# A hybrid decoder layer on one core: the attention's output projection as seven block products, and the stretch behind the attention laid out from tasks

## The chip, the cores and the metric

The kernel runs on 1 core of one Trainium2 chip. The time is the device time of one execution in microseconds, and a kernel's time is the median over its runs. Names of the engines: PE is TensorE (PEld its weight loads), DVE is VectorE, ACT is ScalarE, POOL is GpSimd, SP is SyncE, which issues most DMAs here.

## The reference, cut to what matters

One layer for 512 tokens of width 1024, in float32:

```
h = RMSNorm(x)
[q | k | v | x_rnn | g_rnn | gate_attn | gate_rnn] = h @ W_in
A = differential attention (q and k normalised, shared relative bias, causal), 8 heads of 128 columns
R = GeLU(g_rnn) * RG-LRU(CausalConv4(x_rnn))
x = x + (sigmoid(gate_attn) * (A @ P_attn) + sigmoid(gate_rnn) * (R @ P_rnn)) @ W_out
x = x + relu(RMSNorm(x) @ W_up)^2 @ W_down
```

P_attn, P_rnn and W_out are 1024 x 1024, W_up 1024 x 4096, W_down 4096 x 1024. The change is about `A @ P_attn` and about what is computed between the attention and `@ W_out`.

## The kernel before, in words

**Layout and precision.** Activations lie with the model's width on the partitions and the 512 tokens on the free axis. Each matmul operand is split into a high part (a copy rounded to fp32r, made by ScalarE) and a low part (what is left, by VectorE), and `mm3` (L138) makes a product of three matmuls, high x high, high x low, low x high. The weights come as units of 128 x 1024 floats (512 KB). `Weights.fetch` (L99) has SP load one into one of two `wraw` buffers, `cast` (L106) makes the high part `whi` and the low part `wlo` in one of four slots, and a `wraw` buffer is free for the next load when its low part is made. There are two such streams, `wa` (q, k, v, the gate projections, then P_attn) and `wb` (x_rnn and g_rnn, then P_rnn and W_out); they share buffers and slots.

**Order.** ScalarE, VectorE and GpSimd are called through `InOrder` (L61), so each executes its instructions in the order in which the code emits them; what they record has line L69. Each engine waits at its head instruction with all others queued behind it. TensorE's order is the code's, too.

**Stages.** First the norm and the first gates. Then `attention` (L581): 32 steps, one per head and block of 128 queries, then some more to run out. `acts` holds for each step what is done; heads' projections (`qkv_pair`, L502, one per pair of heads) and the gate projections `ga` are generators from which `fill_in` (L195) takes pieces to keep TensorE at work beside the softmax. `normed_a` and `normed_b` normalise q and k: VectorE sums squares (`ss`, `ms`), GpSimd takes the power -1/2 (`rs`, 128 x 8), VectorE multiplies (`qn`); the halves of q and k change places by DMAs of GpSimd (`qkT`). When a head is through, `post_a` (L654) has ScalarE copy its output from PSUM (`of`) and square it (`osq`), `post_b` has TensorE sum it over partitions with a matmul by `ones` (L666) and GpSimd take the power, `post_c` fetches that power to all partitions (`rb`), and `post_d` scales the head into `aT[h]`, high and low.

Then the **recurrent stretch** (pool `rp`, from about 285 to 500 us): for each of four chunks of 256 channels the products for x_rnn and g_rnn (`cols_proj`, 2 units each), the convolution, GeLU, two gate matmuls per block, and the scan. Its order is written by hand: small jobs are put in `side`, `tick` (L907) takes one after each half unit of TensorE work, and fills in with `fill`, the rest of the gates and then `y_attn` (L846), which is A @ P_attn. `y_attn` takes four groups of 256 output columns, each of 2 units x 8 products of 3 matmuls with 512 columns: 8 units, 192 matmuls, `acc<-aT,whi` and `acc<-aT,wlo` in the profile. When the jobs are done, `y_rnn` (L854) makes R @ P_rnn and merges it with the gated attention part into `mT`. During this stretch GpSimd makes sums of W_up's blocks in DRAM (`weight_sums`, L283), 18 loads into or added onto `sum` and 12 writes, each waiting for the one before; they are for the MLP.

**The MLP**, and W_out before it, stand behind this. The MLP's products are made by a seven-product scheme (Strassen-Winograd: a 2 x 2 block product with 7 instead of 8 block products, from sums of blocks), and its order is laid out by a planner from tasks (`task`, L1034). Neither is changed.

PSUM has 8 banks of 128 x 512 floats: pool `ppa` for the attention (3 `acc`, 5 `at`), `ppb` for the recurrent stretch (6 `acc`, 2 `at` for the small gate matmuls), `ppc` from W_out on (8 `acc`).

Of the kernel before, what the change touches and what calls it, by code (L numbers as in the profile page):

```python
# [39 lines left out]
def tile_block(ctx: ExitStack, tc: tile.TileContext, x, w_in, w_rga, w_rgx, w_pa, w_pr, w_o,  # L40
# [38 lines left out]
    def psum(tag):  # L79
        return pp.tile([P, 512], F32, tag=tag, name=tag, bufs=nb[tag])  # L80
# [7 lines left out]
    class Weights:  # L88
# [4 lines left out]
        def cols(self, w, c0, shift=0, k0=0, n=KT):  # L93
            for k0 in range(k0, k0 + n, 4):
                self.reqs.append((w[k0 // 4, c0 // 256], 4))
                self.shift.append(shift)
            return self

# [157 lines left out]
    OQ, OK_, OV, OX, OG, OGA, OGR = (j * DM for j in range(7))  # L256
    wa = Weights(2, 2)
# [7 lines left out]
    for j in range(4):  # L265
        wa.cols(w_pa, 256 * j, 64)
# [3 lines left out]
    for u in range(2):  # L270
        for j in range(2):
            wb.cols(w_pr, 256 * j, 64, 4 * u, 4)
    for j in range(2, 4):
        wb.cols(w_pr, 256 * j, 64)
# [7 lines left out]

    def weight_sums(behind):  # L283
        t = stg.tile([P, 1024], F32, name="sum")
        G.tensor_copy(t[:, :1], behind[:, :1])
        for n in range(2, 8, 2):
            for blocks in (((0, None), (1, "M5"), (3, "M6"), (2, "M4")), ((1, None), (3, "M7"))):
# [12 lines left out]

    def gate_out(dst, j, ps, rb=None):
        u = unit("gate", F32)
        for c in range(2):
# [5 lines left out]
            dst[2 * j + c] = u[:, c, :]  # L309

# [191 lines left out]
    def qkv_pair(j, qk, v):  # L502
# [22 lines left out]
        def turn(qi, qn, gsc, hh):  # L525
# [17 lines left out]
            else:  # L543
# [3 lines left out]
                for c in range(2):  # L547
                    if False:
                        high(c, halves[1 - c])
                    else:  # L550
                        G.dma_start(d[halves[1 - c], c, :], d[halves[c], c, :])
# [4 lines left out]
        for o, qi, gsc in ((OK_, 1, kg), (OQ, 0, qg), (OV, None, None)):  # L556
            for t, cost in enumerate(proj(o, banks[o])):
# [18 lines left out]
                if j == 0 and o != OK_:  # L576
                    next(bt)
            if o != OV:
                pend = [(qi, qn[o], gsc, 0), (qi, qn[o], gsc, 1)]

    def attention(fills, qks, vs, pads):  # L581
# [72 lines left out]
        def post_a(h):  # L654
            o = st["av", h]
            of = wk.tile([P, S], F32, tag="of", name="of", bufs=2)
            sq = wk.tile([P, S], F32, tag="osq", name="osq")
# [18 lines left out]
        def post_c(h):  # L676
            rb_ = wk.tile([P, S], F32, tag="rb", name="rb")
# [3 lines left out]
        def post_d(h):  # L681
            of = st["of", h][0]
            ov = of.rearrange("e (t p) -> e p t", t=NT)
            V.tensor_tensor(out=ov, in0=ov, in1=st["rb", h].rearrange("e (p t) -> e p t", t=NT), op=ALU.mult)
            aT[h] = unit("aT")
            split(aT[h][:, 0, :], aT[h][:, 1, :], of, sg)
# [6 lines left out]
        for s in range(NH * NT):  # L693
# [8 lines left out]
            if i == 3:  # L702
                at(s + 3, post_a, h)
                at(s + 4, post_b, h)
                at(s + 5, post_c, h)
                at(s + 7, post_d, h)
# [3 lines left out]
        for step in sorted(acts):  # L710
            j = step // (2 * NT)
            if step >= 37:
                wb.pump()
            if step == 30:
                wa.ahead = wa.raws = 1
            if step == 36:
# [4 lines left out]
            while step == NT * NH + 6 and going:  # L721
                next(ga)
# [4 lines left out]
            if step < NT * NH + 6:  # L727
                fill_in(fills[min(j + 1, NH // 2)], pads[min(j, NH // 2)])

    def rnn_chunk(j, rp):  # L730
        def w2(name, dt=F32, bufs=2):
            return rp.tile([P, S], dt, tag=name, name=name, bufs=bufs)

        graw = rp.tile([P, 2, 2, P], F32, tag="graw", name="graw")
        for z, wsrc in enumerate((w_rga, w_rgx)):
            nc.sync.dma_start(graw[:, z], wsrc[2 * j:2 * j + 2].rearrange("n e f -> e n f"))
        gw = [rp.tile([P, 2, 2, P], F32R, tag=f"gw{z}", name=f"gw{z}") for z in range(2)]
        c1 = math.sqrt(2.0 / math.pi)
        d = [dict() for _ in range(2)]
        both = range(2)  # L740
        cw = lambda tap, c: smt[:, C_CW + 8 * tap + 2 * j + c:C_CW + 8 * tap + 2 * j + c + 1]

        def conv(px):
            def head():
                split(gw[0], gw[1], graw)
                for c in both:
                    t = 2 * j + c
                    d[c]["xc"] = w2("xc")
                    A.activation(d[c]["xc"], px[c], AF.Identity, scale=cw(3, c), bias=smt[:, C_CB + t:C_CB + t + 1])
# [856 lines left out]
```

## Time and profile before

| | |
|---|---|
| median of 3 runs | 837.55 us (836.38 to 838.11) |
| the profiled execution, time | 836.64 us |
| its span in the profile | 834.9 us |
| TensorE busy | 828.8 us |
| VectorE busy | 649.6 us |
| ScalarE busy | 479.4 us |
| GpSimd busy | 103.7 us |
| 1-core clock granted to TensorE | 0.999 |

The span is what the hardware profiler saw of the program; the time is 1.7 us longer. A group row reads: line, engine, operation, output <- inputs by the program's names, shapes, xcount | busy us, mean ns of one | idle time of the engine before it and what ended most of that. A row of the timeline is start, duration, engine, line, operation, operands, count, and in brackets the idle time before it and its releaser. A row of DMA issues ends with KB each and the median us from issue to landing. A matmul's recorded duration overlaps its neighbours', so what one costs in a run without holes is the distance between starts.

### The profile page before, as it was taken

To read this page: it belongs to the slowest core of one execution; us is meant where nothing else is said; L and a number is where in the kernel's file an instruction comes from. 1 tells how busy PE (TensorE), PEld (TensorE's weight loads), DVE (VectorE), ACT (ScalarE), POOL (GpSimd) and SP (SyncE) were. 2 spreads that over 40 slices of the span, in tenths; PEclk is the share of its full clock that TensorE was granted. 3 is DMA by queue.
4 is the path that set the end of the run, shared out by engine and by line. 5 is a ranking of instruction groups with operands and counts; after the bars stand their busy time and mean duration, and the time that the engine had idled before them with its cause. 6 is when DMAs were issued, how large, how long until landed. Compare 5 with 4: busy or idle time off the path is not lost.

```text
span 834.9 us, 14382 instructions
## 1 busy us (share of the span) xinstructions
PE 828.8 (99%) x5686; PEld 764.1 (92%) x5686; DVE 649.6 (78%) x1045; ACT 479.4 (57%) x753; POOL 103.7 (12%) x132
## 2 busy tenths in 40 slices
PE   9999999999999999999999999999999999999998
PEld 7899999999988888888888888799999999999998
DVE  6776688988865335978865767899989969977996
ACT  7445475666655335595672345784488448645852
POOL 0042232314111101111110000000000000000000
PEclk9999999999999999999999999999999999999999
DMA  5357332333331347766756672355655576556564
GB/s 203 116 157 224 96 108 79 98 117 89 105 99 39 93 147 202 207 186 190 195 156 179 174 277 76 101 152 151 208 150 148 152 255 174 143 163 202 152 165 114
DMA packets 41173, 126.10 MB, mean 151 GB/s; under 512 B 4993, under 2 KB 9801, under 8 KB 41105
## 3 DMA queue, kind: packets, MB, share of 16 engines
q1 hardware_dynamic: 31152, 92.65, 33.5%
q0 software_dynamic: 9952, 32.53, 17.8%
q8 instruction: 45, 0.74, 0.3%
q14 instruction: 24, 0.19, 0.1%
HBM read 102.05 MB, written 11.05 MB: 135 GB/s over the span
## 4 chain that ended last, share of the span: by engine, by line
PE 76%; DVE 10%; ACT 6%; DMA 4%; issue 3%; SPq 0%; ACTq 0%; DVEq 0%
PE acc L69 37%; PE acc L139 10%; PE acc L140 10%; PE acc L141 10%; DVE wlo L69 3%; PE at L595 2%; ACT whi L69 2%; DMA wraw<-in_w_o_dram 2%; DMA wraw<-in_w_pr_dram 2%; PE at L141 1%; PE at L139 1%; PE at L140 1%; PE at L629 1%; DVE gate L69 1%; ACT q L69 1%
## 5 line engine op out<-in xcount | busy, mean ns | idle before, releaser
L69 ACT CAST whi<-raw 128x1024 fp32r<-128x1024 f32 x109 | 112.1, 1049 | 94.4 <-DVE raw L69 36.8
L69 DVE TENSOR_TENSOR wlo<-wraw,whi 128x1024 fp32r<-128x1024 f32 (+2 forms) x86 | 97.0, 1149 | 75.4 <-ACT whi L69 74.9
L69 PE MATMUL acc<-h,whi 128*128 128x256 f32 (+1 forms) x851 | 154.1, 285 | 0.2 <-DVE h L69 0.2
L69 PE MATMUL acc<-us,whi 128*128 128x256 f32 x900 | 153.2, 276 | 0.0
L69 DVE TENSOR_TENSOR wlo<-raw,whi 128x1024 fp32r<-128x1024 f32 x109 | 130.9, 1219 | 20.4 <-ACT whi L69 20.4
L69 PEld LDWEIGHTS acc<-us,whi 128*128 128x128 f32 x900 | 135.5, 188 | 0.0
L69 PEld LDWEIGHTS acc<-h,whi 128*128 128x128 f32 x851 | 130.7, 188 | 3.3 <-DVE h L69 0.5
L69 PE MATMUL acc<-us,wlo 128*128 128x256 f32 x448 | 123.6, 276 | 0.0
L69 PE MATMUL acc<-h,wlo 128*128 128x256 f32 (+1 forms) x424 | 120.8, 285 | 0.0
L69 ACT CAST whi<-wraw 128x1024 fp32r<-128x1024 f32 (+2 forms) x86 | 82.6, 982 | 53.6 <-DMA wraw<-in_w_in_dram 33.2
L139 PE MATMUL acc<-whi,hT 128*128 128x256 f32 x384 | 107.6, 280 | 0.0
L140 PE MATMUL acc<-wlo,hT 128*128 128x256 f32 x384 | 107.0, 279 | 0.2 <-DVE wlo L69 0.2
L69 PEld LDWEIGHTS acc<-us,wlo 128*128 128x128 f32 x448 | 84.1, 188 | 0.0
L139 PE MATMUL acc<-hT,whi 128*128 128x512 f32 x208 | 81.3, 391 | 0.0
L141 PE MATMUL acc<-hT,wlo 128*128 128x512 f32 x208 | 81.0, 390 | 0.0
L69 PEld LDWEIGHTS acc<-h,wlo 128*128 128x128 f32 x424 | 79.6, 188 | 1.5 <-DVE wlo L69 0.3
L141 PE MATMUL acc<-whi,hT 128*128 128x256 f32 x288 | 80.1, 278 | 0.0
L140 PEld LDWEIGHTS acc<-wlo,hT 128*128 128x128 f32 x384 | 72.3, 188 | 0.7 <-DVE wlo L69 0.4
L139 PEld LDWEIGHTS acc<-whi,hT 128*128 128x128 f32 x384 | 72.3, 188 | 0.4 <-issue 0.2
L69 POOL TENSOR_TENSOR rs<-ms,mhalf 128x8 f32<-128x8 f32 (+1 forms) x25 | 39.3, 1574 | 183.9 <-DVE ms L69 183.9
L69 POOL DMA_DIRECT2D raw<-raw x24 | 20.7, 863 | 324.2 <-DVE raw L69 130.5
L140 PE MATMUL acc<-hT,whi 128*128 128x512 f32 x156 | 60.7, 389 | 0.0
(207 smaller groups left out, 1716.6 us busy)
## 6 DMA issues: line engine op xcount, KB each, us to landing
wraw<-in_w_in_dram SPq DMA_DIRECT2D x54, 512.0 KB, 3.6
raw<-in_w_dn_dram SPq DMA_DIRECT2D x32, 512.0 KB, 4.3
raw<-in_w_up_dram SPq DMA_DIRECT2D x29, 512.0 KB, 4.3
raw<-raw POOLq DMA_DIRECT2D x24, 512.0 KB, 4.6
sum<-in_w_up_dram POOLq DMA_DIRECT2D x18, 512.0 KB, 5.5
wraw<-in_w_pa_dram SPq DMA_DIRECT2D x8, 512.0 KB, 4.4
wraw<-in_w_pr_dram SPq DMA_DIRECT2D x8, 512.0 KB, 4.3
wraw<-in_w_o_dram SPq DMA_DIRECT2D x8, 512.0 KB, 4.5
```

The costliest lines, as they stand in the source:

```text
L69: ins = f(*a, **k)
L139: T.matmul(o, l[0], r[0], start=first, stop=False)
L140: T.matmul(o, l[0], r[1], start=False, stop=False)
L141: T.matmul(o, l[1], r[0], start=False, stop=last)
L595: T.matmul(lg[c][:, :N], qT[:, c, i * P:(i + 1) * P], qk[h % 2, z][:, c, :N], start=z == 1, stop=z == 2)
L629: T.transpose(out=tp[:, b * P:(b + 1) * P], in_=st[s][:, b * P:(b + 1) * P], identity=ident)
```

## The change

1. **A @ P_attn by seven products.** W's layout is changed on the host: `pa4` has for each half n of the output columns four blocks (512 inputs x 256 columns). `add_up` makes the four sums of blocks that the scheme needs (M5, M6, M4, M7) in DRAM for each half, in all 12 loads into or added onto `sum` and 8 writes, on GpSimd, one taken by each `next(pas)`: six in the first `qkv_pair`, then one per step of the attention. `pair_forms` makes the sums of activation blocks for each pair of heads (`af`, `ag`) on VectorE, ScalarE casts them, VectorE makes their low parts. `project` has 7 products per half, each of one weight unit and 24 matmuls with 256 columns: 14 units and 336 matmuls. Their results are copied (`yq`), merged and gated.
2. **The stretch as tasks.** `recurrent` describes each instruction between attention and W_out as a task with an engine, a duration and what it waits for; `Plan` lays them out, tries 400 random changes of ranks, keeps the best, and emits the tasks by planned start. TensorE's order is given by a string: x and g products, y (the seven products), t (gate matmuls), a, b, c (P_rnn in parts), o (the first three units of W_out). The squares of the GeLU are scaled in ScalarE, so that 8 TENSOR_SCALARs of VectorE (`q<-q`) go. The tiles for R, `af` and `ag` share 8 buffers. P_rnn's units come in another order, first the four of the upper input half, then those of the lower.
3. **The attention's end.** The last head's scaling becomes three of those tasks; its `of` and `osq` lie in the `sum` tile. The first `wb` unit is fetched at step 33 instead of 36, and cast from step 34 on instead of 37.
4. **PSUM.** `ppb` has 8 `acc` and serves to the end; `ppc` is gone.

The diff, cut to its core:

```diff
@@ weights and sums
-    for j in range(4):
-        wa.cols(w_pa, 256 * j, 64)
+    pa_sums = [{p: dp.tile([P, 1024], F32, name=f"pa{n}{p}") for p in ("M5", "M7", "M6", "M4")} for n in range(2)]
+    CHAINS = ((0, None), (1, "M5"), (3, "M6"), (2, "M4")), ((1, None), (3, "M7"))
...
+    def add_up(w, into):
+        t = stg.tile([P, 1024], F32, tag="sum", name="sum")
+        for blocks in CHAINS:
+            for b, p in blocks:
+                if p:
+                    G.dma_start(t, w[b], accum_op=ALU.add)
+                    yield
+                    G.dma_start(into[p], t)
+                else:
+                    G.dma_start(t, w[b])
+                yield
@@ qkv_pair
+                if j == 0 and t % 2 == 1:
+                    next(pas)
@@ attention
-            if step >= 37:
+            if step >= 34:
                 wb.pump()
-            if step == 36:
+            if step == 33:
                 wb.fetch()
-            while step == NT * NH + 6 and going:
-                next(ga)
...
+            next(pas, None)
+        post_c(NH - 1)
+        return post_d(NH - 1)
@@ recurrent, pair_forms(i)
+            w = [V_(whole(c), [*(whose if c else ()), before.get(("w", c))]) for c in both]
+            f0 = V_(less("f", 0, (0, 1), (1, 1), tag="tt1"), [*w, before.get("f")], 256)
+            g0 = V_(less("g", 0, (0, 0), (0, 1), tag="ae"), [w[0], before.get("g")], 256)
+            f1 = V_(less("f", 1, ("f", 0), (0, 0)), [f0], 256)
+            g1 = V_(less("g", 1, (1, 0), ("f", 1), ALU.add), [f1, g0], 256)
...
+                a = A_(high(lambda d=d: d(0), s), [after, *w], n)
+                out.append(V_(low(lambda d=d: d(1), s, lambda d=d: d(0)), [a], n))
@@ recurrent, project(n)
+                    for v in range(2):
+                        for i in range(4):
+                            f = form(p, i)
+                            for e, (l, r) in enumerate(((hi, 0), (hi, 1), (lo, 0))):
+                                I.matmul(bank[on][:, 256 * v:256 * v + 256], l[:, i, P * v:P * v + P], f[:, r], start=fresh and v == i == e == 0,
+                                         stop=i == 3 and e == 2, skip_group_check=True)
...
+                t = pe(2.72, product(p, unit, fresh, on), [unit.low, prev[on], *need], [held[on]] if fresh else ())
@@ recurrent, GeLU
-                    A.activation(d[c]["q"], pg[c], AF.Square)
-                    V.tensor_scalar(out=d[c]["q"], in0=d[c]["q"], scalar1=0.044715 * c1, scalar2=c1, op0=ALU.mult, op1=ALU.add)
+                    A.activation(w2(c, "q"), pg[c], AF.Square, scale=math.sqrt(0.044715 * c1))
@@ recurrent, the order of TensorE and the end
+        seq = 'xx gg xx yy g y g tttt y x y x yy g tttt y g y x y x y g tttt y g yy aaa tttt a b c bc bc bc ooo'
...
+        plan.run(dict(zip(("PE", "DVE", "ACT", "SP"), (*(0.0, 1.0, 1.0), 0.0))), 400)
@@ PSUM
-    nb = {"acc": 6, "at": 2}
+    nb = {"acc": 8}
...
-    pp = psum_pool("ppc")
-    nb = {"acc": 8}
```

**TensorE, the projection's matmuls**, before: a piece of `y_attn` (`aT`, here head 0's) behind a piece of a gate projection (`hT`); numbers behind the names are those of the buffers.

```order
L139 MATMUL acc_3671<-hT_82,whi_3607 128x512
L140 MATMUL acc_3671<-hT_82,whi_3607 128x512
L141 MATMUL acc_3671<-hT_82,wlo_3608 128x512
L139 MATMUL acc_3702<-aT_1787,whi_3601 128x512
L140 MATMUL acc_3702<-aT_1787,whi_3601 128x512
```

After: the end of the first product and the beginning of the second.

```order
L69 MATMUL acc_3954<-aT_3407,wlo_3939 128x256
L69 MATMUL acc_3954<-aT_3767,whi_3938 128x256 x2
L69 MATMUL acc_3954<-aT_3767,wlo_3939 128x256
L69 MATMUL acc_3994<-aT_1813,whi_3902 128x256 x2
L69 MATMUL acc_3994<-aT_1813,wlo_3903 128x256
L69 MATMUL acc_3994<-aT_2517,whi_3902 128x256 x2
```

The products have half the columns, and both halves of a bank take one after the other. They begin later in the stretch: the first x_rnn and g_rnn products now stand ahead of them.

**ScalarE, the end of the attention**, before: `pt10` is the last transposed block of probabilities, `of` and `osq` the last head's output and its square, `gate` the gate projections'.

```order
L69 CAST whi_3476<-wraw_3231 128x1024
L69 CAST whi_3493<-wraw_3337 128x1024
L69 CAST pt10_499<-at_3499 128x4x128
L69 COPY of_3530<-at_3458 128x512
L69 ACTIVATE osq_3531<-at_3458 128x512
L69 ACTIVATE aT_3535<-of_3351,sg_456 128x512
L69 ACTIVATE gate_3575<-acc_3480 128x512
L69 ACTIVATE gate_3575<-acc_3538 128x512
L69 CAST whi_3582<-wraw_3497 128x1024
```

After:

```order
L69 CAST whi_3506<-wraw_3261 128x1024
L69 CAST whi_3523<-wraw_3367 128x1024
L69 CAST pt10_507<-at_3531 128x4x128
L69 CAST whi_3550<-wraw_3529 128x1024
L69 COPY of_3568<-at_3488 128x512
L69 ACTIVATE of_3568<-at_3488 128x512
L69 ACTIVATE aT_3572<-of_3381,sg_464 128x512
L69 ACTIVATE gate_3612<-acc_3510 128x512
L69 ACTIVATE gate_3612<-acc_3575 128x512
L69 CAST whi_3616<-wraw_3527 128x1024
```

A cast, of the first x_rnn unit (`wraw_3529`, the second of two loads that SP issues one after the other), now stands ahead of the copy of the last head's output.

**GpSimd, the first half of the attention**, before: `rs8` are the powers for q and k; the four listed are the fourth to the seventh.

```order
L69 DMA qkT_752<-qkT_752 64x512 x2
L69 TENSOR_TENSOR rs8_791<-ms_792,mhalf_80 128x8
L69 DMA qkT_800<-qkT_800 64x512 x2
L69 TENSOR_TENSOR rs8_1039<-ms_1040,mhalf_80 128x8
L69 TENSOR_TENSOR rs8_1139<-ms_1140,mhalf_80 128x8
L69 TENSOR_TENSOR rs8_1233<-ms_1234,mhalf_80 128x8
L69 DMA qkT_1300<-qkT_1300 64x512 x2
```

After, from the same `qkT` on (ahead of it stand two loads into `sum` and one write, each behind one of the first three powers):

```order
L69 DMA qkT_764<-qkT_764 64x512 x2
L69 TENSOR_TENSOR rs8_803<-ms_804,mhalf_80 128x8
L69 DMA qkT_812<-qkT_812 64x512 x2
L69 DMA sum_591<-in_w_pa_dram 128x1024
L69 DMA pa0M6_87<-sum_591 128x1024
L69 DMA sum_591<-in_w_pa_dram 128x1024
L69 DMA pa0M4_88<-sum_591 128x1024
L69 TENSOR_TENSOR rs8_1055<-ms_1056,mhalf_80 128x8
L69 DMA sum_591<-in_w_pa_dram 128x1024 x2
L69 TENSOR_TENSOR rs8_1157<-ms_1158,mhalf_80 128x8
L69 DMA pa0M7_86<-sum_591 128x1024
L69 TENSOR_TENSOR rs8_1252<-ms_1253,mhalf_80 128x8
```

Between the fourth power and the sixth there are now six transfers of 512 KB, and before the fourth three; all use one `sum` tile and wait for each other.

More of the change, by code (lines that the diff above doesn't have):

```diff
@@ L299, in unit @@
         return actp.tile([P, 2, S], dt, tag="unit", name=name)
+    units_of = {}
     def gate_out(dst, j, ps, rb=None):
@@ L726, in attention @@
             next(spg, None)
[L727 to L737, printed above, removed]
-        c1 = math.sqrt(2.0 / math.pi)
[L739 to L749, printed above, removed]
-                if j == 0:
-                    weight_sums(d[0]["xc"])
-            def tap(n):
-                sh = 3 - n
-                for c in both:
@@ new lines, in tile_block, with __init__ @@
+    class Hold:
+        def __init__(self, place, n):
+            self.place, self.n, self.users, self.end = place, n, [], 0.0
+    class Step:
+        def __init__(self, engine, us, go, after, land):
+            self.engine, self.us, self.go, self.after, self.land = engine, us, go, after, us + land
+            self.then, self.start, self.begun, self.frees, self.place = [], None, None, [], 0
+            for x in after:
+                x.then.append(self)
+    LANDS = {"PE": 0.17, "DVE": 0.09, "ACT": 0.09}
@@ L793, in gates @@
[L793 to L808 removed]
+                    b = plan.hold("bank")
@@ new lines, in chunk, with part, go @@
+            new[0]["gates"], new[1]["gates"] = gates_pe[:2], gates_pe[2:]
+            new[0]["gates"] = new[1]["gates"] = gates_pe
+            prior[:] = new
+            gate_pes.append(gates_pe)
+        project(0)
+        project(1)
+        for j in range(4):
+            chunk(j)
+        ps = {}
+        mh = []
+        def part(j, unit, ks, u):
+            def go():
+                if u == 0 and ks[0] == 0:
+                    ps[j] = psum("acc"), psum("acc")
+                hi, lo = unit.pair
+                for k in ks:
+                    kk = 4 * u + k
+                    for c in both:
+                        cs = slice(c * P, (c + 1) * P)
+                        mm3(ps[j][c], (hi[:, k, cs], lo[:, k, cs]), (R[kk][:, 0, :], R[kk][:, 1, :]), kk == 0, kk == 7)
+            return go
@@ new lines, in recurrent @@
+        lates = []
+        w_o_first = []
+        for u in range(3):
+            h = plan.hold("raw"), plan.hold("unit")
+            load = plan.task("SP", 0.1, lambda: wb.fetch_one(), (), 4.4, takes=h[:1])
+            cast = plan.task("ACT", act(1024), lambda: wb.cast(lates), [load], takes=h[1:])
+            low = plan.task("DVE", dve(1024), lambda: lates.pop(0)(), [cast])
+            h[0].users += [cast, low]
+            t = pe(5.44, lambda: None, [low, *w_o_first[-1:], *(m_done[4 * u:4 * u + 4] if u < 2 else ())])
+            h[1].users.append(t)
+            w_o_first.append(t)
```

625 lines of the change are left out of this document (460 added, 165 removed).

## The prediction

> **What bounds the kernel now.** First the page's head: busy time by engine, and the granted clock.
>
> ```profile
> span 834.9 us, 14382 instructions
> PE 828.8 (99%) x5686; PEld 764.1 (92%) x5686; DVE 649.6 (78%) x1045; ACT 479.4 (57%) x753; POOL 103.7 (12%) x132
> PEclk9999999999999999999999999999999999999999
> ```
>
> TensorE is busy for 828.8 of 834.9 us at full clock, so at most about 6 us of the span are idle TensorE. Then its own waits by what ended them (total, times, longest), of which these are the first and the fourth:
>
> ```profile
> PE acc L69 <- DVE zero L69: 1.2, 1, 1.2
> ...
> PE acc L140 <- DVE wlo L69: 0.2, 1, 0.2
> ```
>
> The largest is 1.2 us, once. Then the two stretches that the change touches, attention and the recurrent stretch, in the table by windows (length, busy time and count of PE, PEld, DVE, ACT, POOL, clock, DMA share, GB/s):
>
> ```profile
> 50.00:270.00 220.00, 219.54 (x1697) 209.65 (x1697) 168.48 (x430) 126.31 (x273) 54.04 (x53) 1.00 0.37 110
> 292.00:525.00 233.00, 233.00 (x1030) 192.63 (x1028) 163.76 (x225) 126.73 (x174) 21.02 (x31) 1.00 0.61 178
> ```
>
> In the second, TensorE has no hole in 233 us; VectorE has 163.76 (70%), ScalarE 126.73 (54%). The time is therefore TensorE's work, and it can fall only with that work. Reordering the stretch has nothing to win by itself; it can only keep the others from being late. The chain of waits says the same (76% TensorE), but it wanders through engines that are merely in step, so I take the windows.
>
> **The change part by part.** *The projection's matmuls.* Before, 192 matmuls of 512 columns; after, 14 products of 24 matmuls of 256 columns, 336. The groups of the old ones, and the starts of two solid runs, one of each width:
>
> ```profile
> L139 PE MATMUL acc<-aT,whi 128*128 128x512 f32 x64 | 24.9, 389 | 0.0
> L140 PE MATMUL acc<-aT,whi 128*128 128x512 f32 x64 | 24.9, 389 | 0.0
> L141 PE MATMUL acc<-aT,wlo 128*128 128x512 f32 x64 | 24.7, 389 | 0.0
> ...
> 281.23 0.39 PE L141 MATMUL acc<-hT,wlo 128*128 128x512 f32 x1
> 285.99 0.39 PE L141 MATMUL acc<-hT,wlo 128*128 128x512 f32 x1
> ...
> 751.85 0.39 PE L69 MATMUL acc<-us,whi 128*128 128x256 f32 x2
> 752.87 0.39 PE L69 MATMUL acc<-us,whi 128*128 128x256 f32 x2
> ...
> L69 PEld LDWEIGHTS acc<-us,whi 128*128 128x128 f32 x900 | 135.5, 188 | 0.0
> ```
>
> The 389 ns overlap their neighbours, so the price is the pitch between starts. From 281.23 to 285.99 there are 21 steps: 4.76/21 = 0.2267 us at 512 columns. From 751.85 to 752.87 there are 9 matmuls (in threes, two of them in one row): 1.02/9 = 0.1133 us at 256, exactly half, although each weight load lasts 188 ns: the loads overlap. So 192 x 0.2267 = 43.53 us become 336 x 0.1133 = 38.07: **-5.44 us**, all of it on the path, since TensorE is the path. The rest of its work in the stretch is the same in number and shape.
>
> *What VectorE and ScalarE take on*, by rows of 292 to 525 us:
>
> ```profile
> L69 DVE TENSOR_TENSOR wlo<-wraw,whi 128x1024 fp32r<-128x1024 f32 x38 | 45.8, 1224 | 51.9 <-ACT whi L69 51.6
> L69 DVE SCALAR_TENSOR_TENSOR gate<-gate,acc 128x512 f32<-128x512 f32 x16 | 10.7, 681 | 0.1
> L69 DVE TENSOR_TENSOR xl<-xc,xh 128x512 fp32r<-128x512 f32 x8 | 5.2, 686 | 0.1
> L69 DVE TENSOR_SCALAR q<-q 128x512 f32<-128x512 f32 x8 | 3.1, 422 | 0.3 <-ACT q L69 0.2
> L69 DVE TENSOR_TENSOR fs<-q 128x256 f32<-128x256 f32 x6 | 2.5, 418 | 0.0
> L69 ACT CAST whi<-wraw 128x1024 fp32r<-128x1024 f32 x38 | 38.8, 1042 | 41.2 <-DMA wraw<-in_w_in_dram 25.9 <-DMA wraw<-in_w_pr_dram 13.2 <-DMA wraw<-in_w_o_dram 2.1
> L69 ACT CAST xh<-xc 128x512 fp32r<-128x512 f32 x8 | 4.7, 618 | 3.4 <-DVE xc L69 3.4
> L69 ACT ACTIVATE q<-acc 128x512 f32<-128x512 f32 x8 | 4.4, 593 | 0.2 <-DVE R L69 0.2
> L69 ACT ACT_TABLE_LOAD x7 | 9.0, 1283 | 0.1
> L69 ACT ACTIVATE tt<-at,hb 128x512 f32<-128x512 f32 x16 | 10.1, 679 | 0.0
> L69 ACT ACTIVATE ae<-tt,sp 128x512 f32<-128x512 f32 x8 | 6.5, 809 | 0.0
> ```
>
> VectorE: 6 more lows, 6 x 1.224 = 7.3; the activations' forms, per pair of heads three passes of 512 and six of 256 columns, 4 x (3 x 0.686 + 6 x 0.418) = 18.3; 14 merges and gatings for 8 gatings, 6 x 0.681 = 4.1; less the 8 TENSOR_SCALARs, 3.1. Together +26.6, so 190 us in a stretch of 227.6: 84%. ScalarE: 6 casts, 6.3; forms' casts, 4 x (0.618 + 2 x 0.41) = 5.8 (0.41 at 256 columns is an estimate on the line through 512 and 1024); 6 copies, 3.6. Together 142 us, 63%. Neither becomes the bound by its sum, and TensorE's work covers all of it as long as the order fits. If it did not, the 26.6 us would show in part.
>
> Whether the order fits I judged by walking the new order with these durations against a TensorE without holes. VectorE stands 2 to 10 us ahead with each weight's low half, with these exceptions, counted from the first x product: at +116 us the x product's second bank waits for a tanh, before which ScalarE must, once the matmuls for the first gate end at +112.2, do a copy, a table load, a tanh, an exponential and a cast, 0.59 + 1.28 + 0.68 + 0.81 + 1.04 = 4.4, then the tanh itself, 0.68: about 0.3 us late, part of it overlapped; at +126 us a gate product waits for the last convolution tap in a bank that it takes over, 0 to 0.3 us late; at +45 and near the end the lead is 1.4 and 1.9 us. I take **+0.5 us**; bounds 0, if each lead is as walked, and +3.6, worked out under the rivals. None is below nothing, since TensorE has no hole there to close.
>
> *The end of the attention.* Before, ScalarE copied and squared the last head's output, then TensorE's matmul with ones took it:
>
> ```profile
> 271.07 0.59 ACT L69 CAST pt<-at 128x512 fp32r<-128x512 f32 x1 [0.83 <-PE at L629]
> 275.31 0.59 ACT L69 COPY of<-at 128x512 f32<-128x512 f32 x1 [3.65 <-PE at L141]
> 275.80 0.60 ACT L69 ACTIVATE osq<-at 128x512 f32<-128x512 f32 x1
> 277.78 0.95 PE L666 MATMUL at<-ones,osq 128*128 128x1 f32 x8
> L103 SPq DMA_DIRECT2D wraw<-in_w_in_dram x2: 327/328/328, 270.6 to 271.7; - x2
> wraw<-in_w_in_dram SPq DMA_DIRECT2D x1, 512.0 KB, 4.8
> ```
>
> The square ends at 276.40, and the matmul starts at 277.78: a lead of 1.38 us. In the new order of ScalarE the cast of the recurrent stretch's first weight (its fetch is now at step 33, its cast from step 34 on) stands ahead of that copy. The second load of the pair, issued at 271.7, carries this weight in the new order of SP; it took 4.8 (the last row is of that one alone), so it lands at about 276.5. The cast waits for that, 1.04; the copy, 0.5, and the square, 0.6, are queued behind: 278.7. The ones matmul is next on TensorE and everything is in order behind it: 278.7 - 277.78 = **+0.9 us**. Bounds: nothing if the load takes the 3.5 us of its partner, +2 if 6. Later in the old order the same cast found its load landed; nothing is won back, since it was hidden there.
>
> *The sums of weight blocks.* 20 transfers of 512 KB, all on POOL's in-order queue within the attention, each waiting there for the one before, and POOL also makes the powers `rs` that the normalisation of q and k waits for. Rows: POOL's first power, the sixth, what takes the sixth on VectorE; the same kind of chain for the MLP's weights, first and last of its 30 transfers; and transfers that were slower:
>
> ```profile
> 52.39 1.65 POOL L69 TENSOR_TENSOR rs<-ms,mhalf 128x8 f32<-128x8 f32 x1 [4.10 <-DVE ms L69]
> 97.14 2.48 POOL L69 TENSOR_TENSOR rs<-ms,mhalf 128x8 f32<-128x8 f32 x1 [8.21 <-DVE ms L69]
> 102.41 0.69 DVE L69 TENSOR_TENSOR qn<-acc,rs 128x512 f32<-128x512 f32 x1
> ...
> 311.92 0.54 POOL L69 DMA_DIRECT2D sum<-in_w_up_dram  x1 [0.30 <-POOL sum L69]
> 471.64 0.56 POOL L69 DMA_DIRECT2D up6M<-sum  x1 [6.69 <-DMA sum<-in_w_up_dram]
> x<-in_x_dram SPq DMA_DIRECT2D x4, 512.0 KB, 8.2
> wraw<-in_w_pa_dram SPq DMA_DIRECT2D x7, 512.0 KB, 4.8
> ```
>
> From the first issue to the last there are 29 steps: 159.72/29 = 5.5 us each. From 54.0, where the first power ends, eight such steps stand ahead of the sixth power in the new order: 54.0 + 44 = 98, and the issue of the next, 0.9, so it starts at 98.9 instead of 97.14. Its result is taken 102.41 - 99.62 = 2.79 us after its end, so 1.8 us late is hidden. The other powers and the copies of q and k have leads of 4 us and more by the same count. I take **+0.3** for the traffic beside the weight loads; bounds 0 and +7 (the slower rival).
>
> *Without a price:* w_pa's six additional loads hang on SP with the others (4.8 us each, room for them in the walk); eight banks for six and two, and one PSUM pool for two, change no instruction; the last head's scaling has VectorE's lead of some 20 us before the product that takes it.
>
> *Sum.* The profiled execution took 836.64 us (1.7 above its span); 836.64 - 5.44 + 0.9 + 0.5 + 0.3 = 832.9. The median of the three runs shown, 837.55, is 0.9 above the profiled one, the mean of all four 0.5; with 0.6 added, **833.5 us**.
>
> By the Trainium skill (TensorE: Matmul & The Clock Gate, section Back-to-back issue gap) a stream of weight loads and matmuls is spaced by both, about 81 ns at 128 columns and 131 at 512. By that, an estimate: 192 x 0.131 = 25 us would become 336 x 0.081 to 0.131 = 27 to 44 us, 2 to 19 us worse. The trace has 0.2267 and 0.1133 instead, and they decide.
>
> **The rivals.** *All covers hold* (the load quick, no tight place late): 836.64 - 5.44 + 0.6 = 831.8. For it: the leads are estimates of 0 to 0.9 us late. Against: the cast stands ahead of the copy for certain, and only a load a microsecond quicker hides it. 0.14; from 831.3 to 832.4.
>
> *The saving is eaten in the recurrent stretch.* With VectorE at 84%, a weight that lands late is not caught up at once. The loads had 4.8 us, the slowest kind of transfer there 8.2: 3.4 later, less the lead of 1.4 to 1.9 at the two narrow places, is 1.5 to 2 each time; two such are 3.6 us: 832.9 - 0.5 + 3.6 + 0.6 = 836.6. For it: 63 to 84% busy. Against: TensorE never once waited there at 70%. 0.24, from 834.6 to 838.
>
> *POOL's queue holds the attention up* (slower than before). The place is the sixth power. It decides from (2.79 - 1.8)/8 = 0.12 us more per transfer, and each further 0.1 us per transfer costs 0.8 us. At 6.5 us each the power is 9.8 us late and VectorE, which works in order, stands for 7.0; behind it TensorE, whose waits there were near nothing: 833.5 - 0.3 + 7.0 = 840.2. For it: 8.2 us has been seen. Against: the attention moves 110 GB/s where the stretch with 5.5 us moved 178. 0.10, from 838.5 to 844.
>
> *The weight load sets the pace*, so that the change does not do what it says: if 256-column matmuls were spaced by the 188 ns of their load, 336 x 0.188 = 63.2 us for 43.5: 836.64 + 19.6 + 2.3 = 858.5. The skill's rule above points this way. Against: 0.1133 us, with the same loads. 0.02.
>
> **How the numbers follow.** My forecast has 0.50, from 832.4 to 834.6. What can be told from no change is 0.2%, 1.7 us: faster is below 835.9, slower above 839.2. The forecast and the first rival (0.64) are faster, and half of the second (0.12): 0.76. The other half and a fifth of the third: 0.14 the same. The rest of the third and the last: 0.10. From 831.3 the forecast and the first rival hold 0.64; two thirds of the second, up to 837.0, bring 0.80.
>
> **What would show it.** TensorE's group of 256-column matmuls grows by 336 and its busy time falls by about 5.4 us; TensorE has one hole of 0.9 us at about 278 before the ones matmul, ended by ScalarE's square; waits of a few tenths at 116 and 126 us after the first x product; VectorE near 84% in the stretch; POOL's sixth power near 99 us and no wait of VectorE for `rs` over 1 us. I am wrong if TensorE waits more than 3 us in all in the stretch, if VectorE waits for `rs`, or if the pitch is above 0.114 us.

## The result: 1.2% slower, and the profile after

| | before | after |
|---|---|---|
| median | 836.52 us (835.9 to 838.11, 6 runs) | 847.68 us (844.77 to 850.67, 6 runs) |
| the profiled execution | 836.64 us | 848.73 us |
| ratio, 95% interval | | 1.0123 (1.0106 to 1.0140) |

The change makes the kernel 11 us slower. The head of the changed kernel's page:

```profile
span 846.9 us, 14784 instructions
PE 829.6 (98%) x5830; PEld 768.3 (91%) x5830; DVE 673.9 (80%) x1085; ACT 494.4 (58%) x777; POOL 118.6 (14%) x152
```

TensorE is busy for 829.6 us, 0.8 more than before, where the prediction had 5.4 less. But the span less that is 17.3 us where it was 6.1: most of the time went into holes. TensorE's waits by what ended them, the first two (total, times, longest):

```profile
PE acc L69 <- ACT h L69: 3.8, 1, 3.8
PE acc L69 <- ACT whi L69: 2.1, 1, 2.1
```

`h` is the MLP's normalised input and the `whi` of 2.1 belongs to the MLP as well: both lie behind the stretch that the change rewrites. The windows of the attention, of the stretch, and of the passage from W_out into the MLP, after:

```profile
50.00:270.00 220.00, 216.32 (x1669) 205.87 (x1668) 167.14 (x427) 123.27 (x268) 69.36 (x73) 1.00 0.56 156
292.00:525.00 233.00, 231.88 (x1180) 197.15 (x1178) 181.34 (x253) 138.33 (x193) 20.51 (x31) 1.00 0.65 190
500.00:540.00 40.00, 35.71 (x148) 28.23 (x147) 30.30 (x45) 24.07 (x35) 0.00 (x0) 0.96 0.28 85
```

and the last of them before:

```profile
500.00:540.00 40.00, 39.77 (x174) 32.29 (x173) 32.54 (x47) 24.69 (x40) 0.88 (x1) 1.00 0.30 91
```

The attention has lost 3.2 us of TensorE work, the stretch 1.1, the passage 4.1, with a clock of 0.96 there. Windows at fixed times shift against the work, so I keep a ledger: the start of one and the same matmul in both timelines, the difference being how far the changed kernel is behind. Up to the end of the attention matmuls are counted from the first, behind the stretch from the last, since the change alters their number only in between. The places where it jumps are the ones matmul (before at 277.78, as shown) and, before:

```profile
518.39 0.39 PE L140 MATMUL acc<-tail,whi 128*128 128x512 f32 x1
751.40 0.28 PE L69 MATMUL acc<-us,wlo 128*128 128x256 f32 x1
754.23 0.56 PE L69 MATMUL acc<-h,whi 128*128 128x384 f32 x3
```

and after:

```profile
283.50 0.72 PE L696 MATMUL at<-ones,of 128*128 128x1 f32 x5 [0.71 <-ACT of L69]
522.44 0.39 PE L152 MATMUL acc<-tail,whi 128*128 128x512 f32 x1
761.45 0.28 PE L69 MATMUL acc<-us,wlo 128*128 128x256 f32 x1
766.60 0.56 PE L69 MATMUL acc<-h,whi 128*128 128x384 f32 x3
```

The ones matmul is 283.50 - 277.78 = 5.7 us late, W_out 4.05, the MLP 10.05, and behind a hole that follows at 761.45 it is 766.60 - 754.23 = 12.37. In full, for all kernels (e1 to e12 are the experiments below; each column is what that part of the program adds; the profiled executions, against before's). A row is a single execution, up to 3.6 us from its kernel's median, and parts with the same code differ between rows: the attention with the changed kernel's sums has +3.5 to +6.9 (without what is lost at the start), the passage from W_out into the MLP, where it is not edited, +4.0 to +6.0.

| kernel | attention | its end | stretch | W_out to MLP | MLP | all |
|---|---|---|---|---|---|---|
| after | +4.85 | +0.97 | -1.76 | +5.99 | +2.32 | +12.37 |
| e1 no sums | -0.23 | +1.05 | -1.33 | +4.04 | +2.03 | +5.56 |
| e2 copies | -0.64 | +0.78 | -2.40 | +4.31 | +1.75 | +3.80 |
| e3 offset 64 | +5.35 | +0.81 | -0.13 | +4.63 | +1.44 | +12.10 |
| e4 fetch first | +3.52 | +0.76 | -1.49 | +1.66 | +2.84 | +7.29 |
| e5 spread | +0.30 | +0.74 | +0.18 | +4.11 | +1.96 | +7.29 |
| e6 later cast | +4.29 | -0.02 | +0.34 | +4.57 | +1.50 | +10.68 |
| e7 short warm-up | +8.88 | +0.76 | -2.38 | +5.96 | +1.24 | +14.46 |
| e8 e4, e5, e6 | -0.40 | -0.01 | +1.16 | +1.70 | +2.25 | +4.70 |
| e9 five edits | +0.49 | -0.01 | +0.35 | -0.04 | +2.06 | +2.85 |
| e10 before with sums | +6.44 | 0.00 | -0.07 | -0.81 | +0.73 | +6.29 |
| e11 e9, shifted | +21.21 | -0.01 | -0.65 | +0.31 | +1.10 | +21.96 |
| e12 e9, one matmul more | -0.25 | -0.01 | -0.47 | -0.07 | +0.47 | -0.33 |

In e7 and e11, 1.96 and 20.79 of the attention's column are lost at the start, which these two edit.

### The profile page after: what moved, and what is told of

It is laid out like the page before. It is cut to its first block, busy times and chain, and to the rows that moved or that the text cites. A ratio compares the mean times of both kernels' runs of the same rounds, so it can differ in the third digit from the quotient of the medians.

```text
span 846.9 us, 14784 instructions
## 1 busy us (share of the span) xinstructions
PE 829.6 (98%) x5830; PEld 768.3 (91%) x5830; DVE 673.9 (80%) x1085; ACT 494.4 (58%) x777; POOL 118.6 (14%) x152
## 4 chain that ended last, share of the span: by engine, by line
PE 70%; DVE 11%; DMA 7%; issue 6%; ACT 5%; POOL 2%; SPq 0%; ACTq 0%; DVEq 0%; POOLq 0%
PE acc L69 47%; PE acc L151 5%; PE acc L152 5%; PE acc L153 5%; DVE wlo L69 3%; ACT whi L69 2%; DMA sum<-in_w_pa_dram 2%; PE at L621 2%; PE at L152 1%; POOL rs L69 1%; PE at L153 1%; PE at L151 1%; DMA wraw<-in_w_pa_dram 1%; DVE gate L69 1%; DMA wraw<-in_w_o_dram 1%
## 5 line engine op out<-in xcount | busy, mean ns | idle before, releaser
L69 DVE TENSOR_TENSOR wlo<-wraw,whi 128x1024 fp32r<-128x1024 f32 (+2 forms) x92 | 104.9, 1152 | 54.5 <-ACT whi L69 54.1
L69 ACT CAST whi<-wraw 128x1024 fp32r<-128x1024 f32 (+2 forms) x92 | 89.9, 987 | 52.8 <-PE acc L69 17.3
L151 PEld LDWEIGHTS acc<-whi,hT 128*128 128x128 f32 x384 | 72.2, 188 | 1.4 <-issue 1.1
L69 PE MATMUL acc<-hT,whi 128*128 128x512 f32 x224 | 71.7, 390 | 0.2 <-ACT tt L69 0.2
L69 ACT ACTIVATE pe<-pe,nm 128x128 f32<-128x128 f32 (+3 forms) x64 | 35.6, 559 | 43.6 <-DVE nm L69 43.3
L69 POOL TENSOR_TENSOR rs<-ms,mhalf 128x8 f32<-128x8 f32 (+1 forms) x25 | 41.2, 1650 | 115.7 <-DVE ms L69 115.6
L153 PEld LDWEIGHTS acc<-whi,hT 128*128 128x128 f32 x288 | 54.1, 188 | 0.0
```

The lines of the kernel that those rows point to most:

```text
L69: ins = f(*a, **k)
L151: T.matmul(o, l[0], r[0], start=first, stop=False)
L153: T.matmul(o, l[1], r[0], start=False, stop=last)
```

## The experiments

**The attention: the sums' transfers, by traffic or by waiting?** VectorE's waits for the powers from 48 to 172 us, after:

```profile
DVE qn L69 <- POOL rs L69: 7.3, 5, 2.0
```

e1 takes the transfers out (the products that took sums multiply a plain block, so the output is no longer the layer's):

```diff
-    unit = Unit(w_pa[n, PLAIN[p]] if p in PLAIN else pa_sums[n][p], 0)
+    unit = Unit(w_pa[n, PLAIN.get(p, 1)], 0)
-    pas = chain(*(add_up(w_pa[n], pa_sums[n]) for n in range(2)))
+    pas = (None for _ in range(99))
```

> Leaves out the 20 transfers on GpSimd's queue in the attention; the eight products that took sums take a plain block of the weights instead, so the output is not the reference's, with all other instructions as in the changed kernel. Theory 1 (the sums hold the attention up): TensorE, 5.1 us behind by 172 us in the changed kernel, is level with the kernel before up to the end of the attention, and the time falls by 5 us, to about 842.5. Rival (the attention is late for another reason, such as the order of ScalarE at its end): the 5.1 us stay, about 847.5.

842.24 us, ratio 1.0072 (1.0045 to 1.0098); the attention is level. The transfers cost the 5 us. e2 puts as many transfers of the same size at the same places of GpSimd's queue, with none waiting for another (the products as in e1):

```diff
+    def copies():
+        for m in range(20):
+            G.dma_start(dp.tile([P, 1024], F32, name=f"cp{m}"), w_pa[m % 2, m % 4])
+            yield
+    pas = copies()
```

> As e1_no_sums, but with 20 transfers of 512 KB from DRAM to DRAM at the same places on GpSimd's queue, none of which waits for another; the output is not the reference's. If the cause is that GpSimd waits at the head of its queue for one transfer to land before it issues the next, with the powers queued behind: level in the attention, as e1, about 842.5. If it is the traffic (loads of q, k and v weights that land later): still about 5 us behind, about 847.5.

842.29 us, 1.0061 (1.0042 to 1.0081); attention level. Its DMA issues from 48 to 172 us, and VectorE's waits, which are now those of before, row for row:

```profile
cp<-in_w_pa_dram POOLq DMA_DIRECT2D x20, 512.0 KB, 5.3
```

```profile
DVE qn L69 <- POOL rs L69: 1.8, 1, 1.8
```

So twenty transfers of that size may run beside the attention; that GpSimd stands still for them is what costs. The copies go from DRAM to DRAM and add nothing, so their kind changed too; e5 leaves the kind as it is. It keeps the chain and leaves more time between its links:

```diff
-                if j == 0 and t % 2 == 1:
+                if j == 0 and t == 3:
-            next(pas, None)
+            if step % 2 == 0:
+                next(pas, None)
```

> The same 20 transfers, all waits kept, but taken by GpSimd at every second step of the attention (and three in the first projections) instead of six in the projections and one per step. Theory (a power is late only where GpSimd's queue stands at a transfer whose predecessor has not landed): with about twice the time between two of them, little of the 5.1 us is left at the end of the attention, 0 to 1.5 us, time about 843 to 844. Rival (20 such transfers cost the attention that much wherever they stand): 5 us stay, 848.

843.68 us, 1.0074 (1.0050 to 1.0099); one wait of 1.8 us, attention +0.30. And e10 puts the sums alone, unused, into the kernel before (`add_up`, `pas` and its two `next` as in the change):

> The kernel before, nothing changed but that the 20 transfers stand on GpSimd's queue in the attention where the changed kernel has them; what they write is not used. Theory (the queue alone makes the loss): 5.1 us behind at the end of the attention and to the end, 842. Rival (the loss needs other parts of the change beside it): under 2 us.

842.27 us against a kernel without them, 1.0049 (1.0030 to 1.0067): the attention's loss is there in full, +6.4, with 7.3 us of waits in 5, without any product, task or plan of the change.

**The end of the attention: is the early cast a loss?** e6 casts the first weight at the old step:

```diff
-            if step >= 34:
+            if step >= 37:
```

> The cast of the first weight of the recurrent stretch from step 37 on, as before, instead of 34; TensorE's order is the same. Theory (ScalarE stands at that cast until its load lands, with the copy and the square of the last head behind it): TensorE's hole of 0.9 us ahead of the matmul with ones at 282 goes, the lag grows by 0 instead of 1.0 us there; in all 1 us less. Rival (the hole comes from the last head's tiles, which now lie in the tile of the sums, or from VectorE): it stays.

848.08 us, 1.0128 (1.0102 to 1.0154): the hole at 282 us is gone, and nothing is won. TensorE in e6, 14 us later:

```profile
298.39 0.73 PE L69 MATMUL acc<-hT,whi 128*128 128x512 f32 x2 [1.62 <-ACT whi L69]
299.65 0.50 PE L69 MATMUL acc<-hT,wlo 128*128 128x512 f32 x1 [0.53 <-DVE wlo L69]
```

Now the first x product waits for its weight, since ScalarE has to cast two in a row there. The cast of step 34 costs 0.97 and spares 2.2. Step 35 (in e9) has neither hole.

**W_out to the MLP.** SP's issues of the residual `x`, before:

```profile
481.28 2.25 SPq L957 DMA_DIRECT2D x<-in_x_dram  x4
```

and after, with those of W_out's next units behind them; then the VectorE instructions, and from the chain of waits the transfer, that hang on them:

```profile
488.15 1.75 SPq L1370 DMA_DIRECT2D x<-in_x_dram  x4
490.00 1.31 SPq L115 DMA_DIRECT2D wraw<-in_w_o_dram  x2
```

```profile
488.54 1.22 DVE L69 TENSOR_TENSOR wlo<-wraw,whi 128x1024 fp32r<-128x1024 f32 x1
498.43 1.23 DVE L69 TENSOR_TENSOR wlo<-wraw,whi 128x1024 fp32r<-128x1024 f32 x1 [7.47 <-ACT whi L69]
499.57 1.28 DVE L69 TENSOR_TENSOR x<-acc,x 128x512 f32<-128x512 f32 x2
```

```profile
490.00 7.25 DMA wraw<-in_w_o_dram
```

The plan ends with the merge into `mT`. It has put the third W_out unit's low part behind all of that merge, at 488.54, so the `wraw` buffer that the fifth unit's load needs is free only at 488.54 + 1.22 = 489.76. And `x` takes the place of a tile that the merge still reads, so SP holds the loads of `x` until 488.15, and they too stand ahead of that load, which is issued at 490. It takes 7.25 us beside the four of `x`, and VectorE, in order, stands 7.47 us for its low part. The first sum of `x` starts at 499.57; before it was at 488.62:

```profile
488.62 1.28 DVE L69 TENSOR_TENSOR x<-acc,x 128x512 f32<-128x512 f32 x2
```

VectorE never makes the 11 us up, and where TensorE has finished W_out and what it could do ahead, it runs dry:

```profile
529.88 0.39 PE L69 MATMUL acc<-h,wlo 128*128 128x512 f32 x1
534.03 1.52 PE L69 MATMUL acc<-h,whi 128*128 128x512 f32 x2 [3.76 <-ACT h L69]
535.35 0.63 PE L69 MATMUL acc<-h,wlo 128*128 128x512 f32 x1
535.77 1.05 PE L69 MATMUL acc<-h,whi 128*128 128x512 f32 x2
536.63 0.63 PE L69 MATMUL acc<-h,wlo 128*128 128x512 f32 x1
537.05 0.73 PE L69 MATMUL acc<-h,whi 128*128 128x512 f32 x2
```

From 529.88 to 534.03 is 4.15, 3.92 more than the usual 0.2267; then six starts take 537.05 - 534.03 = 3.02 instead of 1.36, another 1.7. Together 5.6 of the ledger's 5.99. e4 only has SP issue the next W_out load ahead of most of `x`:

```diff
+    wb.fetch()
     (ahead of the loads of x)
```

> One more W_out unit is asked for ahead of the four loads of x, so that on SP it no longer stands behind all four. Theory (the fifth unit's load, held behind the loads of x and beside them, is what VectorE waits 7.5 us for at 490, and all sums for the MLP come 6 us late): the unit lands about 3 us earlier, the wait of VectorE falls to 4 us, TensorE's hole at 530 from 3.9 to about 1 us with little of the slow start behind it, about 844 in all. Rival (the loads of x themselves, issued at 488 instead of 481, set the pace): they now come later still, no gain, 848.

847.2 us (its profiled execution 843.58), 1.0121 (1.0087 to 1.0154): the low part comes at 493.85, the hole is 1.7 us and the clock stays at 1.00; this part costs 1.66 instead of 5.99, and the whole execution is not told apart from after's by its median. The place is right, but not all of the gain is the edit's. From the third unit's low part to the fifth's it is 493.85 - 485.03 = 8.82 us, after 498.43 - 488.54 = 9.89: 1.1 less. The load still waits for its buffer, until 486.28, and only has one load of `x` ahead of it instead of four. And after's profiled execution is a costly one: one of its W_out loads, issued at 467.41, took 8.7 us (in e7, 5.96, one took 8.6), and its merge ended some 2 us later against TensorE than in e1, e2, e3, e5 and e6, which leave this part as it is and pay 4.04 to 4.63. Against these e4 saves 2.4 to 3.0, more than the 1.1, since no slow starts follow its shorter hole. The 1.7 that is left goes with the plan's end (e9).

**Three mends at once.** e8 has the edits of e4, e5 and e6.

> Three edits together: the sums at every second step (e5_spread), the cast from step 37 on (e6_pump37), and one more W_out unit asked for ahead of the loads of x (e4_fetch_first). If the three causes are separate, their gains add: 847.7 - 4.5 - 1 - 4 = 838, still not faster than before. If the parts only hide one another, it stays above 841.

844.67 us, 1.0071 (1.0047 to 1.0095), more than expected. Attention and its end are mended, but the hole of e6 comes along and the stretch is 1.2 us longer than before's. So e9 takes step 35, and tells the planner what it could not see, that the last merges may come behind the third unit's low part; with offset 192 for the products' weights as a second try on the pitch:

```diff
-            if step >= 34:
+            if step >= 35:
-    unit = Unit(w_pa[n, PLAIN[p]] if p in PLAIN else pa_sums[n][p], 0)
+    unit = Unit(w_pa[n, PLAIN[p]] if p in PLAIN else pa_sums[n][p], 192)
+                if j == 3:
+                    last_posts.append(x)
...
+            for x in last_posts:
+                x.after.append(low)
+                low.then.append(x)
     (and the edits of e4 and e5)
```

> The changed kernel with five edits, one for each loss: sums at every second step; the cast of the stretch's first weight from step 35 on, so behind the copy and square of the last head but not at step 37; the low half of the third W_out unit ahead of the last posts of mT, and one more W_out unit asked for ahead of the loads of x; the units of the seven products 192 bytes into their tile. Theory (each loss has its own place): level in the attention, no hole over 0.3 us at 278, none over 0.5 us at 291, TensorE's hole ahead of the MLP below 0.5 us, 1 to 1.5 us left in the MLP: 836.9 - 5.4 + 2.2 + 1.5 = 835.2, and 1.4 less if the offset of 192 bytes brings the pitch to 113.3. Rival (with VectorE at 84% a wait that is taken away comes back at another place of the stretch): 840 or more.

837.92 us (12 runs) against 837.46 (18), 1.0006 (0.9993 to 1.0020): level with before. SP and VectorE in e9:

```profile
476.67 2.62 SPq L115 DMA_DIRECT2D wraw<-in_w_o_dram  x2
```

```profile
489.50 1.37 DVE L69 TENSOR_TENSOR x<-acc,x 128x512 f32<-128x512 f32 x2 [1.50 <-PE acc L153]
```

The load of 490.00 is now the second of the two that are issued from 476.67 on, since the third unit's low part is no longer behind the merge; the first sum of `x` is 0.9 us behind before's, and the passage costs nothing. e9 has the edit of e4 too; the new edge of the plan alone was not run. With every loss outside the stretch but the MLP's mended, the change still wins nothing: its own stretch gives +0.35. Of the 5.44 us that were to be saved there, the longer pitch (0.120 us in e9, see below) takes some 2.3, and four waits of TensorE, at 325, 377, 413 and 438 us, take 2.7 more.

**The stretch: the pitch.** After, two runs of products:

```profile
326.31 0.38 PE L69 MATMUL acc<-aT,wlo 128*128 128x256 f32 x1 [0.56 <-DVE wlo L69]
327.89 0.28 PE L69 MATMUL acc<-aT,whi 128*128 128x256 f32 x1
...
337.10 0.40 PE L69 MATMUL acc<-af,whi 128*128 128x256 f32 x2
339.92 0.40 PE L69 MATMUL acc<-xh,gw 128*128 128x512 f32 x1
```

From 326.31 to 327.89 are 14 starts, 1.58/14 = 0.1129 us. From 337.10 to 339.92 are 24, 2.82/24 = 0.1175. Only the first two products have the predicted pitch; the other 288 matmuls take 0.1177 in the mean, 4.4 ns more, 1.3 us. Two ideas about why: the place of a weight within its tile (e3), and an opening with an odd width, since the MLP's runs at 0.1133 begin with one of 384 columns (e12).

```diff
-    unit = Unit(w_pa[n, PLAIN[p]] if p in PLAIN else pa_sums[n][p], 0)
+    unit = Unit(w_pa[n, PLAIN[p]] if p in PLAIN else pa_sums[n][p], 64)
```

> One number: the weight units of the seven products begin 64 bytes into their tile, as all other units of that stretch and the eight units of the projection before, instead of at its start. If the place decides the pitch of those 256-column matmuls: 117.6 ns becomes 113.3, 336 x 4.3 ns = 1.4 us less, about 846. If the pitch comes from the activations' tiles or from the change of banks: 117.6 stays, no difference beyond 0.3 us in the stretch.

850.39 us, 1.0169 (1.0134 to 1.0203): the pitch is 119.8 ns, longer. With 192 (e9) it is 120.4. The place acts, but the wrong way. e12 is e9 with offset 0 and

```diff
+                    if fresh:
+                        x = early[0].rearrange(...)[:, 0] if p == "M5" else aT[p == "M2"][:, 0, :]
+                        I.matmul(bank[on][:, :384], hi[:, 0, :P], x[:, :384], start=True, stop=True)
```

> e9_five with the units of the seven products at the start of their tile (as in the changed kernel), and one matmul of 384 columns ahead of each product that begins a bank (6 of 14), as the MLP has it at some of its products; it is overwritten. Theory (the pitch of 256-column matmuls depends on how they fall in after the 512-column ones, and 384 columns set it right): 113.3 ns in the six products and what follows them directly, 117.6 in the others. Rival (it comes from where the operands lie in memory): 117 to 120 in all 14. The time itself: level with e9_five, 837 to 838.

838.43 us (10 runs), 1.0013 (0.9998 to 1.0028). Behind the opening with 384 columns:

```profile
334.18 0.28 PE L69 MATMUL acc<-aT,wlo 128*128 128x256 f32 x1
336.77 0.63 PE L69 MATMUL acc<-hT,whi 128*128 128x512 f32 x2
```

22 steps, 2.59/22 = 0.1177. The idea falls; offset 0 is the best of three. What puts the first two products, or the MLP's, at 0.113 stays open; e7, with the same stretch and offset, has no product at it, and e5 has the last two.

**The MLP's hole.** Its weights' sums hang on GpSimd's chain of `raw<-raw` transfers, of which the 18th took 4.8 us before and 6.2 after. A transfer of instructions falls into it both times; the DMA of that time, before and after:

```profile
q8 instruction: 1, 0.02, 1.1%
raw<-raw POOLq DMA_DIRECT2D x1, 512.0 KB, 4.8
```

```profile
q8 instruction: 1, 0.02, 1.8%
raw<-raw POOLq DMA_DIRECT2D x1, 512.0 KB, 6.2
```

Before, the instructions come 4.3 us behind the issue, just ahead of the landing; after, 1.5 us behind it. e7 and e11 shift where they fall, by other numbers of matmuls at the start (1 instead of 17; 112 with 2 columns more, in e9).

```diff
-        for n in range(17):
+        for n in range(1):
```

> One matmul instead of 17 ahead of the norm, so that TensorE's stream is 32 instructions shorter ahead of the MLP. The change has 144 more pairs of weight load and matmul there, 288 instructions, 32 more than one instruction transfer of 16 KB carries at 64 bytes each, so from the first weights of the MLP on the transfers of instructions come at the places of the kernel before again. Theory (the hole of 2.3 us at 761 comes from an instruction transfer that meets the 18th of GpSimd's accumulating transfers, 6.2 us instead of 4.8): that transfer takes 4.8 again and the hole goes, 2 us less there; the start may lose up to 2 us. Rival (the hole comes from the late start of the MLP): it stays.

849.58 us, 1.0133 (1.0105 to 1.0160); the transfer takes 5.0, the hole is 1.24 instead of 2.32.

```diff
+        for n in range(112):
+            I.matmul(pw[:, :2], zero[:, :P], zero[:, :2], start=True, stop=True)
```

> e9_five with 112 more matmuls of 2 columns behind the 17 at the start, 224 instructions, so that with the 288 of the change TensorE's stream is 512 longer ahead of the MLP: two instruction transfers of 256, and these come at the places of the kernel before again. The start is later by some us, the rest is e9_five. Theory (an instruction transfer beside GpSimd's 18th accumulating transfer makes that 6 us long and TensorE wait 1.9 us at 752): the transfer takes 4.5 to 5.0 us and the hole is below 0.7 us. Rival (the hole comes with the MLP's start or the seam): 1.5 to 2 us stay.

857.64 us, 1.0248 (1.0229 to 1.0268), of which the additional matmuls at the start take 20.8; the transfer takes 4.7 (e9: 6.2), the hole is 1.10 (e9: 2.06). In all fourteen profiles one transfer of instructions falls into the 18th: 4.3 to 4.6 us behind its issue in before, e7, e10 and e11, where it takes 4.7 to 5.0, and 1.3 to 3.0 us behind it in the other ten, where it takes 5.6 to 6.2. So the moment and the length go together. The hole does not follow from the length alone: e3, with nothing shifted, loses 1.44 with 5.7 us, e12 0.47 with 5.6. In after TensorE waits for a load of W_up that SP issues only behind that transfer, at 756.00, and that takes 4.65 (in e11 5.35). Of the 2.32 us, 6.2 - 4.8 = 1.4 can be the transfer's; the rest is open. That the MLP begins late is not the cause: in e10 it begins 5.6 us late and loses nothing at this place (its 0.73 come later).

## Why the prediction was wrong, point by point

**"-5.44 us, all of it on the path": the sign right, the size wrong.** The number of matmuls and the path were right. The pitch came from the MLP, 0.1133; here it was 0.1177 in the mean for 288 of 336, which leaves -4.17. Before had both paces in its own attention, at 256 columns:

```profile
75.77 0.28 PE L141 MATMUL acc<-whi,hT 128*128 128x256 f32 x1
77.53 0.28 PE L141 MATMUL acc<-whi,tail 128*128 128x256 f32 x1
...
78.57 0.28 PE L139 MATMUL acc<-whi,hT 128*128 128x256 f32 x1
82.54 0.28 PE L141 MATMUL acc<-whi,hT 128*128 128x256 f32 x1
```

15 steps are 1.76/15 = 0.1173, then 35 are 3.97/35 = 0.1134. One run of rows does not give a pitch; I took the lower of two that stood in the trace, as if there were one. A pitch "above 0.114" was named as a sign of error, and it came.

**"I take +0.5 us" for stalls in the stretch: too little, at the named places and at another.** The tanh came as walked (0.32 us at 416 us). A low part of the first product, at 325.5, was 0.72 late, and at 449 the gate matmuls lost 0.71. With these 1.75 in all, the matmuls' -4.17 would be -2.42; the ledger has -1.76, and the remaining 0.66 is spread in steps too small to place. VectorE at 78% of the window (181.34 of 233) and ScalarE at 59% did not become bounds, as said.

**"+0.9 us" at the end of the attention: right, 0.97, by the mechanism given.** ScalarE after: the cast waits for its load, and the copy stands behind it, with the square behind that.

```profile
281.41 1.05 ACT L69 CAST whi<-wraw 128x1024 fp32r<-128x1024 f32 x1 [4.90 <-DMA wraw<-in_w_in_dram]
282.37 0.58 ACT L69 COPY of<-at 128x512 f32<-128x512 f32 x1
```

"Nothing is won back" holds against the kernel before, where no matmul waited for that cast. In the new order it is not the whole of it: without the early cast, e6 loses 2.2 us at the first x product.

**"I take +0.3" for the sums: the step that failed in the attention, +4.85.** It was the mechanism of the rival with 0.10, and the sixth power came late by that rival's own rule; but the sixth is one of four that did. GpSimd after: the first transfer, the fifth power, and the sixth with the issue ahead of it; then VectorE at the fifth:

```profile
53.45 0.75 POOL L69 DMA_DIRECT2D sum<-in_w_pa_dram  x1
...
95.62 1.68 POOL L69 TENSOR_TENSOR rs<-ms,mhalf 128x8 f32<-128x8 f32 x1
...
102.43 0.88 POOL L69 DMA_DIRECT2D sum<-in_w_pa_dram  x1 [3.57 <-DVE pe L69]
103.01 2.80 POOL L69 TENSOR_TENSOR rs<-ms,mhalf 128x8 f32<-128x8 f32 x1
```

```profile
97.33 0.69 DVE L69 TENSOR_TENSOR qn<-acc,rs 128x512 f32<-128x512 f32 x1 [1.97 <-POOL rs L69]
```

Eight steps, from 53.45 to 102.43, are 48.98/8 = 6.1 us each, not 5.5; the rival decides from 5.62. The power at 97.14 starts at 103.01, 5.9 late against a lead of 2.79. The fifth, before at 87.26, starts at 95.62, 8.4 late against a lead of 6.6, and VectorE waits for it 1.97 us, then 1.54 for the sixth, 0.42 for the eighth and 1.56 for the tenth; a wait of 1.83 for the first power was there before, too. TensorE's lag grows by 1.2 us behind the fifth power, 1.5 behind the sixth and 1.9 behind the tenth. The 5.5 was the mean of a chain elsewhere. Here the first two transfers that are added onto took 9.4 us, issued at 58.42, and 11.1, issued at 73.06:

```profile
sum<-in_w_pa_dram POOLq DMA_DIRECT2D x1, 512.0 KB, 11.1
```

And the argument against the rival, that the attention moved less per second than the stretch (110 GB/s against 178), averaged over 220 us what is decided in the first 50. Before's DMA from 50 to 82 us:

```profile
DMA packets 2707, 6.88 MB, mean 215 GB/s; under 512 B 384, under 2 KB 392, under 8 KB 2704
```

The other powers' leads "of 4 us and more" were counted with the same 5.5.

**What the sum did not hold: +5.99 and +2.32.** The sum stopped where the rewritten stretch stops. W_out's and the MLP's instructions were unchanged, but what supplies them was not: SP's order, and where VectorE stood when the stretch ended. Without these 8.31 us the kernel would still be 12.37 - 8.31 = 4.06 slower, since the attention and its end cost more than the stretch gains; they make up two thirds of the whole. The place and the mend of the first are shown (e4, e9); the second is open in part.

*The sum again:* -4.17 (matmuls) + 1.75 + 0.66 (the rest of the stretch) + 0.97 + 4.85 + 5.99 + 2.32 = 12.37, the ledger's total; the span has 12.0, as what follows the last matmul is 0.4 shorter.

## What to carry to other kernels

A chain of transfers on the queue of an engine that also makes something small is paid in that engine's waits: price each link by the slowest transfer of its own time, and check every result of the engine, not one. Where a plan or a rewritten stretch ends, follow each queue, and each buffer, to the first thing behind it that must be on time; the plan cannot see that, and here one edge to it, with one load moved, took away a passage of 4 to 6 us. And a pitch is read from several runs of rows: here one width had four.

## What the hardware showed that I had not expected

After the hole of 3.76 us TensorE ran four starts in 537.05 - 535.35 = 1.70, 0.425 us each, at 512 columns, against 0.2267, and the window's clock was 0.96; after the 1.7 us of e4 it was 1.00. By the Trainium skill (TensorE: Matmul & The Clock Gate, section Part 1: The HAM clock gate) an idle window of some 3.4 us halves the clock, to N/1.2 ns, 427 at 512 columns. The pace agrees; the length does not: in e5 TensorE is idle for only 2.63 us at that place, the starts behind it take 0.427 as well, and the window's clock is 0.96, too:

```profile
500.00:540.00 40.00, 37.34 (x157) 30.06 (x156) 31.17 (x47) 25.03 (x38) 0.00 (x0) 0.96 0.29 93
```

In the fourteen profiles each of TensorE's eight idle times of 2.6 to 3.8 us behind the start of the kernel was followed by 3.4 us at a granted clock of 0.50 (after: from 533.9 to 537.3), and none of up to 2.5 us was. In after that cost 1.7 us on top of the hole.

256-column matmuls with the same shapes ran at 0.1129, 0.1175, 0.1198 and 0.1204 us by run and by the weight's place in its tile. The transfers of 512 KB that were added onto took from 4.5 to 11.1 us in the changed kernel. And the changed kernel's executions spread by 5.9 us (844.77 to 850.67), those of before by 2.2; only one execution of each is profiled, so no run here shows why.
